# Two quarters of a token-major product turned back by DMA instead of on TensorE, and four squares moved behind their parts

## The chip, the cores and the metric

The kernel runs on one core of one Trainium2 chip. The metric is the device time of one execution in microseconds. Five engines work side by side, each through its own queue in order: TensorE (PE; its weight loads are shown as PEld), VectorE (DVE), ScalarE (ACT), GpSimd (POOL) and SyncE (SP), which here only issues DMAs. The order of the instructions in each queue is fixed when the program is built.

## The reference, cut to what matters

Two layers; each is a feed-forward block, a mixing block and a second feed-forward block, with a norm ahead of each and one at the end. All is float32, with 512 tokens, width 1024 and inner width 2816.

```python
def swiglu(h, w_gate, w_up, w_down):
    return (jax.nn.silu(h @ w_gate) * (h @ w_up)) @ w_down

for l in range(DEPTH):
    x = x + 0.5 * swiglu(rms_norm(x, ffn1_norm[l]), ffn1_wg[l], ffn1_wu[l], ffn1_wd[l])
    h = rms_norm(x, mix_norm[l])
    z = h @ w_in[l]
    ...            # window attention and short convolution of z
    x = x + jnp.concatenate([attn_out, conv_out], axis=-1) @ w_out[l]
    x = x + 0.5 * swiglu(rms_norm(x, ffn2_norm[l]), ffn2_wg[l], ffn2_wu[l], ffn2_wd[l])
return rms_norm(x, final_norm)
```

## The kernel before

**Layout.** The state `x` lies feature-major: eight blocks `xs[c]` of 128 features by 512 tokens, two of them to a tile `xpair[m]`. Every float32 factor is split into a high part (a cast to fp32r, on ScalarE) and a low part (the rest, by a subtraction on VectorE; line 223 does both), and a product is three matmuls: high by high, high by low, low by high. So weights come in by DMA as `raw`, become `wh` (ScalarE) and `wl` (VectorE), three buffers of each, and TensorE runs over them. `need_split` and `take_split` keep this up a fixed number of steps ahead, in the order of `plan()`.

**Seven products for eight.** The large products are taken in 2 x 2 blocks with seven block products instead of eight (`CHAINS`, `SHARES`). The feed-forward's stages are listed in `FIRST`, `INNER` and `LAST`: "p" and "w" make activations, "s" is a part of the down product (`share`) done by seven, and "d" a plain part of it (`down`). `INNER` is used by the second feed-forward of layer 0 and by the first of layer 1. It ends with two "s" stages and `("d", (9, 10))`.

**The product that lies apart.** In these "s" stages the result is token-major: `Apart.add` collects it in tiles `apart` (128 tokens by 512 features), and it must be turned before it can be added to `x`. It has four quarters `(o, t)`: feature half o, token half t. Two ways back are there:

- by DMA: `send` copies each of the two tiles of a quarter on ScalarE into `halves`, with the two 16-bit halves of the words laid apart (line 138), and issues one DMA transpose per tile on SP (line 901); `back` later copies the turned halves together on ScalarE, twice per quarter (line 914), and VectorE adds the result to `x` (line 918);
- on TensorE: `back` turns a quarter with eight transposes of 128x128 into PSUM (line 924), and VectorE adds it from there (line 929).

Before, quarters (0,0) and (1,1) go by DMA: sent behind steps 3 and 4 of the second "s" stage. Quarters (1,0) and (0,1) go over TensorE. Quarters (1,1) and (1,0) come back behind step 6, that is ahead of the "d" stage, and (0,0) and (0,1) behind its first block.

**The last "d" stage and the norm.** `down` yields the eight blocks of x in the order 4, 5, 6, 7, 0, 1, 2, 3, each after 12 matmuls. VectorE adds each to `xs[c]` (line 1318), and `after(c)` prepares the next norm: `take` makes the scaled high part (ScalarE, line 476) and low part (VectorE, line 477), `square` the square (ScalarE, lines 482 and 485) that VectorE accumulates in `nacc` (line 486). The norm's consumer starts with groups of 24 matmuls over the eight parts (line 321 to 324), in the same order of blocks, before the sum of squares is known; the split sum enters TensorE during the second group (`ssq`, line 542), and the root that comes of it scales the results afterwards. Behind the first site the results are gated, and their activation is split (`a`) for the next "d" stage; behind the second they become queries, keys and values.

What a line of Python issues is placed by a scheduler of the framework at build time, after its own estimates; `tc.issue_after` and `tc.manual_schedule` bind it. So the order on each engine can differ from the order of the source.

Of the kernel before, what the change touches and what calls it, by code (L numbers as in the profile page):

```python
# [16 lines left out]
P = 128  # L17
# [7 lines left out]
KC = D // P  # L25
NT = S // P
EPS = 1e-6
FAR = -3.0e38
H = S // 2
# [22 lines left out]
SHARES = ((0, 0, 1), (0, 0, 1), (1, 0, -1), (1, 1, 1), (1, 1, -1), (1, 0, 1), (0, 1, 1))  # L52


SENT_AT = {3: (0, 0), 4: (1, 1)}
SCORES_AT = (5, 6, 7, 8, 9, 10, 12, 13)
TURN_AT = (6, 7, 8, 10, 11, 12, 14, 15)
VALUES_AT = (7, 8, 9, 11, 12, 13, 15, 16)
# [14 lines left out]
def trunk_kernel(  # L73
# [23 lines left out]
    nc = tc.nc  # L97
# [8 lines left out]
    def psum(tag, shape, name):  # L106
        return ps.tile(shape, F32, tag=tag, bufs={"mm": 4, "sc": 2, "aux": 2}[tag], name=name)

    def g2(name, dt=F32, shape=(P, S)):
        return work.tile(list(shape), dt, tag="g2", bufs=14, name=name)  # L110
# [21 lines left out]
    def words(ap):  # L132

        return ap.bitcast(U16).rearrange("p (n two) -> p two n", two=2)
# [30 lines left out]
    ident = const.tile([P, P], F32, name="ident")  # L165
# [8 lines left out]
    def turn_rows(i):  # L174
        n = rows[i].shape[0]
        rp = psum("aux", [P, n], f"par_ps{i}")
        nc.tensor.transpose(rp, rows[i], ident[:n, :n])
        nc.scalar.copy(par[:, 16 * i : 16 * i + n], rp)
# [15 lines left out]
    state = {"raw": 0, "split": 0, "group": 0, "late": None}  # L194
# [153 lines left out]
    def halves_of(n, wide, last):  # L348

        blocks = list(range(0, n, wide))  # L350
        return blocks[len(blocks) // 2 :] + blocks[: len(blocks) // 2] if last else blocks

    def down(rhs, fresh=False, last=False):

        wide = abreast(len(rhs))
        for c in halves_of(KC, wide, last):
            n, hi, lo = take_split()
            if fresh and c == 0:
                yield from enumerate(level(n, hi, lo, rhs, wide))
                continue  # L360
            for j in range(wide):
                cols = slice(j * P, (j + 1) * P)
                own = (f"{n}_{j}", hi[:, :, cols], lo[:, :, cols])
                tag = ("sc", "sc", "aux", "aux")[j] if fresh else "mm"
                yield c + j, group(rhs, own=own, tag=tag)
# [515 lines left out]
    class Apart:  # L881
# [21 lines left out]
                    halves.rearrange("p a n -> p (a n)"),  # L903
                )

        def back(self, o, t, tag="mm"):

            for m in range(2 * o, 2 * o + 2):
                part = xpair[m][:, :, t * H : (t + 1) * H]
                if (o, t) in self.sent:  # L910
                    whole = g2(f"back_{self.name}_{m}_{t}")
                    j = 2 * (m - 2 * o)
                    with tc.issue_after(state["cast"]):
                        nc.scalar.copy(
                            words(whole).rearrange("p two (c s) -> p two c s", c=2),
                            self.sent[o, t][:, :, j : j + 2, :],
                        )
                    nc.vector.tensor_add(part, part, whole.rearrange("p (c s) -> p c s", c=2))
                    continue
                tp = psum(tag, [P, 2, H], f"back_{self.name}_{m}_{t}")  # L920
                for j in range(2):
                    c = (2 * m + j) % NT
                    for u in range(2):
                        nc.tensor.transpose(
                            tp[:, j, u * P : (u + 1) * P],
                            self.y[2 * t + u, o][:, c * P : (c + 1) * P],
                            ident,
                        )
                nc.vector.tensor_add(part, part, tp)

    def ahead(ops, at):
        return lambda step: ops.make(*at.get(step, ()))


    def ffn(norm, stages, after=None, late=None):
# [4 lines left out]
        def plain(b):  # L940
# [36 lines left out]
            acts[b] = (hi, lo)  # L977

        def winograd(b, between):


# [56 lines left out]
        def winograd2(b, between=None):  # L1038
# [14 lines left out]
            for step, (acc, operand, start) in enumerate(CHAINS):  # L1053
# [38 lines left out]
                if between:  # L1092
                    between(step)
# [115 lines left out]
        def shared(b):  # L1209
            return Seven(lambda: [raws[b], raws[b + 2]], room_form, f"s_{norm.i}_{b}")  # L1210

        def joined(between):


            def step(n):
                if n == 3:
                    crossing[0].join_half(0)
                if n == 4:
                    crossing.pop(0).join_half(1)
                if crossing and isinstance(crossing[-1], Tail):  # L1220
                    crossing[-1].during(n)
                between(n)

            return step
# [17 lines left out]
        def flush(n=1, *tag):  # L1242
            for _ in range(n):
                if pending:
                    pending.pop(0)(*tag)
# [3 lines left out]
        apart = None if first else Apart(f"{norm.i}")  # L1249
        for i, (what, b) in enumerate(stages):  # L1250
            if what in "wu" and stages[i + 1][0] == "s":
                ops = shared(sevens[0])
                if what == "w":
                    winograd2(b, ahead(ops, {3: ("b11",), 4: ("b21",), 5: ("t2",), 6: ("t3",)}))
                else:
                    winograd(b, ahead(ops, {1: ("b11",), 2: ("b21",), 4: ("t2",), 6: ("t3",)}))
            elif what == "w":
                if after is None and b == 1:
                    end = apart = Finale()
                winograd2(b, end and b == 1 and end.step)  # L1260
            if what == "s" and end:
                ends = [
                    Seven(full, None, f"e_{n}")
                    for n, full in enumerate((lambda b=b: [raws[b + 4], raws[b + 6]], raws[b + 8]))
                ]

                def between(step):
                    if 0 < step < 3:
                        flush(2, "mm")
                    for at, n, operand in ((3, 0, "b11"), (4, 1, "b11"), (5, 0, "t2"), (6, 1, "t2")):  # L1270
                        if step == at:
                            ends[n].make(operand)

                share(ops, 0.5, joined(between), apart, still=kept)
            elif what == "e":
                end.last(ends, kept)
                return
            elif what == "s" and b == sevens[0]:
                then = shared(sevens[1])
                share(  # L1280
                    ops,
                    0.5,
                    joined(ahead(then, {3: ("b11",), 4: ("b21",), 5: ("t2",), 6: ("t3",)})),
                    apart,
                    behind=(0, 2, 3) if first else (),
                    still=kept,
                )
            elif what == "s" and i + 1 == len(stages):
                share(then, 0.5, after.step, on=kept)
            elif what == "s":  # L1290

                def between(step):
                    if step in (2, 4):
                        with tc.issue_after(state["rest"]):
                            crossing[0].parts(step // 2 - 1)
                    if step in SENT_AT:
                        apart.send(*SENT_AT[step])
                    if step == 6:
                        apart.back(1, 1)
                        apart.back(1, 0, "aux")  # L1300

                share(then, 0.5, between, apart, behind=(0, 2, 3), on=kept)
            if what == "p":
                plain(b)
                if b == 0 and late:
                    turn_rows(1)
            if what != "d":
                continue
            rhs = [(acts[k][0][:, j, :], acts[k][1][:, j, :]) for k in b if k in acts for j in range(2)]
            final = i + 1 == len(stages)  # L1310
            if final:
                after.norm.order = halves_of(KC, 1, True)
            for c, acc in down(rhs, b == (0,) and not first, final):
                if b == (0,):
                    made = {0: "t3", 4: "t1"} if first else {0: "b21", 2: "t2", 5: "t3"}
                    if c in made:
                        norm.make(made[c])
                nc.vector.scalar_tensor_tensor(
                    xs[c], acc, 0.5, xs[c], op0=ALU.mult, op1=ALU.add
                )  # L1320
                flush()
                if final and c == KC // 2:
                    apart.back(0, 0)
                    apart.back(0, 1, "sc")
                if final:
                    after(c)
            if b == (0,) and first:
                norm.make("t4", "b22")
            if b == (1,) and late:
                late()  # L1330
# [426 lines left out]
```

## Time and profile before

| | us |
|---|---|
| median of 3 runs | 1648.56 (1648.53 to 1649.81) |
| profiled execution | 1648.68 |
| its span | 1646.9 |
| TensorE busy in the span | 1634.7 |
| VectorE busy | 1376.2 |
| ScalarE busy | 1107.6 |

A row of the timeline gives the start in us from the span's start, the duration, engine, line, operation and output<-input with their shapes; `x8` at its end means eight in one row, and a bracket tells how long the engine was idle before and for whom it waited. Instructions of VectorE and ScalarE overlap a little, so that the step from one start to the next is some 0.1 us shorter than the duration; TensorE's matmuls overlap more. In the view of one tile the figures behind a group are the least, median and greatest duration in ns, then the first and last start.

### The profile page before, as it was taken

What the parts mean: (1) busy time and instruction counts of PE and PEld (TensorE: products, weight loads), DVE (VectorE), ACT (ScalarE), POOL (GpSimd) and SP (SyncE); (2) the same over time, 40 slices, a digit from 0 to 9 for tenths busy, and PEclk for the clock granted to TensorE, in tenths of its full rate; (3) what the DMA queues carried; (4) which work ended last, traced back from release to release, by engine and by line L of the source; (5) the groups of instructions that cost most, each with busy time, mean ns of one, the idle gap of its engine ahead of it and who ended that gap; (6) DMA issues with size and microseconds to landing.
All of it is one profiled execution on the core that took longest, in us unless ns stands there. A gap on an engine that the chain in (4) does not pass through costs nothing.

```text
span 1646.9 us, 22039 instructions
## 1 busy us (share of the span) xinstructions
PE 1634.7 (99%) x8076; PEld 1380.4 (84%) x8076; DVE 1376.2 (84%) x1812; ACT 1107.6 (67%) x1453; POOL 212.3 (13%) x188
## 2 busy tenths in 40 slices
PE   9999999999999999999999999999999999999998
PEld 7888889988898888887888888878888988888886
DVE  7987779988899877797999777979788998777997
ACT  6447776566567577777665777776565766777665
POOL 0011111100221111111011111110012111111121
PEclk9999999999999999999999999999999999999999
DMA  8379997741397699999866999998124977999992
GB/s 256 83 199 212 221 245 186 175 126 52 105 235 176 176 216 218 214 204 236 217 151 177 219 216 225 213 230 204 52 65 129 231 152 186 220 224 224 234 262 70
DMA packets 277280, 306.10 MB, mean 186 GB/s; under 512 B 93804, under 2 KB 162484, under 8 KB 277172
## 3 DMA queue, kind: packets, MB, share of 16 engines
q1 hardware_dynamic: 236580, 222.24, 47.1%
q0 software_dynamic: 39872, 81.80, 28.8%
q8 instruction: 63, 1.03, 0.2%
q10 hardware_dynamic: 720, 0.66, 0.1%
q14 instruction: 45, 0.37, 0.1%
HBM read 262.71 MB, written 2.10 MB: 161 GB/s over the span
## 4 chain that ended last, share of the span: by engine, by line
PE 90%; DVE 5%; ACT 2%; issue 2%; DMA 1%; SPq 0%; DVEq 0%; ACTq 0%
PE x L827 25%; PE y L827 13%; PE acc L321 8%; PE acc L322 8%; PE acc L324 8%; PE w L827 6%; PE x_m L812 3%; PE x_s L827 3%; PE x_s L812 2%; DVE wl L223 2%; PE w_s L827 1%; PE y_s L812 1%; PE y_m L812 1%; PE y_e L827 1%; PE acc L707 1%
## 5 line engine op out<-in xcount | busy, mean ns | idle before, releaser
L223 ACT CAST wh<-raw 128x1024 fp32r<-128x1024 f32 (+1 forms) x491 | 510.9, 1044 | 367.6 <-PE x L827 91.9
L223 DVE TENSOR_TENSOR wl<-raw,wh 128x1024 fp32r<-128x1024 f32 (+1 forms) x491 | 594.5, 1219 | 174.6 <-ACT wh L223 173.6
L321 PE MATMUL acc<-xh,wh 128*128 128x512 f32 x424 | 165.8, 393 | 0.0
L322 PE MATMUL acc<-xl,wh 128*128 128x512 f32 x424 | 165.5, 390 | 0.0
L324 PE MATMUL acc<-xh,wl 128*128 128x512 f32 x416 | 162.3, 390 | 0.0
L218 POOL DMA_DIRECT2D raw<-in_ffn_wu_dram x39 | 48.7, 1248 | 400.0 <-DMA raw<-in_ffn_wu_dram 328.5
L322 PEld LDWEIGHTS acc<-xl,wh 128*128 128x128 f32 x424 | 79.7, 188 | 15.9 <-DVE xl L502 0.2
L321 PEld LDWEIGHTS acc<-xh,wh 128*128 128x128 f32 x424 | 79.8, 188 | 15.6
L324 PEld LDWEIGHTS acc<-xh,wl 128*128 128x128 f32 x416 | 78.1, 188 | 16.4
L218 POOL DMA_DIRECT2D raw<-in_ffn_wg_dram x39 | 48.3, 1264 | 222.9 <-DVE raw L262 70.8
L218 POOL DMA_DIRECT2D raw<-in_ffn_wd_dram x34 | 41.0, 1206 | 251.4 <-DMA raw<-in_ffn_wd_dram 80.4
L262 DVE TENSOR_TENSOR raw<-raw,raw 128x1024 f32<-128x1024 f32 x56 | 68.1, 1220 | 2.0 <-DMA raw<-in_ffn_wu_dram 1.1
L1158 ACT COPY raw_a<-turned 128x1024 uint16<-128x1024 uint16 x48 | 63.0, 1355 | 0.0
L827 PE MATMUL x<-wh,ft2h 128*128 128x512 f32 x152 | 59.2, 390 | 0.0
L827 PE MATMUL y<-wh,ft3h 128*128 128x512 f32 x152 | 59.2, 390 | 0.0
L827 PE MATMUL w<-wh,fb21h 128*128 128x512 f32 x152 | 59.2, 390 | 0.0
L827 PE MATMUL x<-wh,ft1l 128*128 128x512 f32 x152 | 59.2, 389 | 0.0
L827 PE MATMUL w<-wl,fb21h 128*128 128x512 f32 x152 | 59.2, 389 | 0.0
L827 PE MATMUL x<-wh,ft1h 128*128 128x512 f32 x152 | 59.2, 389 | 0.0
L827 PE MATMUL x<-wl,ft1h 128*128 128x512 f32 x152 | 59.2, 389 | 0.0
L827 PE MATMUL x<-wl,ft2h 128*128 128x512 f32 x152 | 59.2, 389 | 0.0
L827 PE MATMUL x<-wh,fb22l 128*128 128x512 f32 x152 | 59.2, 389 | 0.0
(607 smaller groups left out, 4625.0 us busy)
## 6 DMA issues: line engine op xcount, KB each, us to landing
raw<-in_ffn_wu_dram SPq DMA_DIRECT2D x126, 512.0 KB, 5.4
raw<-in_ffn_wd_dram SPq DMA_DIRECT2D x105, 512.0 KB, 6.2
raw<-in_ffn_wg_dram SPq DMA_DIRECT2D x86, 512.0 KB, 5.2
raw<-in_ffn_wu_dram POOLq DMA_DIRECT2D x39, 512.0 KB, 8.4
raw<-in_ffn_wg_dram POOLq DMA_DIRECT2D x39, 512.0 KB, 6.8
raw<-in_w_in_dram SPq DMA_DIRECT2D x36, 512.0 KB, 3.7
raw<-in_ffn_wd_dram POOLq DMA_DIRECT2D x34, 512.0 KB, 9.8
raw<-raw POOLq DMA_DIRECT2D x21, 512.0 KB, 7.0
```

Of the source, the lines that this page charges most:

```text
L218: nc.gpsimd.dma_start(out=r, in_=rows_of(*more), accum_op=ALU.add)
L223: return nc.scalar.copy(hi, raw), eng.tensor_sub(lo, raw, f32(hi))
L262: nc.vector.tensor_add(a11, a11, s1)
L321: nc.tensor.matmul(acc, hi[:, k, :], rhs[k][0], start=k == first, stop=False)
L322: nc.tensor.matmul(acc, hi[:, k, :], rhs[k][1], start=False, stop=False)
L324: nc.tensor.matmul(acc, lo[:, k, :], rhs[k][0], start=False, stop=k == last)
L707: nc.tensor.matmul(opening[n], (lo if part == "w" else hi)[:, k, :], xl if part == "x" else xh, start=n not in begun, stop=k == KC - 1 and ...
L812: nc.tensor.matmul(accs[c // 2][:, c % 2, :], w[:, k, cols], x_[:, 2 * h + k, :], start=start and c % 2 == 0 and h + k + i == 0, stop=h + ...
L827: nc.tensor.matmul(accs[u], x_[:, 2 * h + k, tok], w[:, k, :], start=start and h + k + i == 0, stop=h + k == 2 and i == 2, skip_group_chec ...
L1158: nc.scalar.copy(words(raws[self.b][:, c, :]), self.to[:, :, c, :])
```

## The change

All four quarters go by DMA. Quarter (1,0) is sent behind step 5 and (0,1) behind step 6. Only (1,1) still comes back ahead of the "d" stage; (1,0) comes back behind its block 5, (0,0) behind block 6, and (0,1) behind block 0. Blocks 4 and 5 are prepared for the norm behind block 5, blocks 6 and 7 each behind itself. For blocks 0 to 3 the source takes the scaled parts as each block is ready and the four squares only behind block 3.

```diff
-SENT_AT = {3: (0, 0), 4: (1, 1)}
+
+SENT_AT = {3: (0, 0), 4: (1, 1), 5: (1, 0), 6: (0, 1)}
+BACK_AT = {5: (1, 0), 6: (0, 0), 0: (0, 1)}
+FINAL_AT = {5: (4, 5), 6: (6,), 7: (7,)}
...
-        def back(self, o, t, tag="mm"):
+        def back(self, o, t):
 
             for m in range(2 * o, 2 * o + 2):
                 part = xpair[m][:, :, t * H : (t + 1) * H]
-                if (o, t) in self.sent:
-                    whole = g2(f"back_{self.name}_{m}_{t}")
...
-                    continue
-                tp = psum(tag, [P, 2, H], f"back_{self.name}_{m}_{t}")
-                for j in range(2):
-                    c = (2 * m + j) % NT
-                    for u in range(2):
-                        nc.tensor.transpose(
-                            tp[:, j, u * P : (u + 1) * P],
-                            self.y[2 * t + u, o][:, c * P : (c + 1) * P],
-                            ident,
-                        )
-                nc.vector.tensor_add(part, part, tp)
+                whole = g2(f"back_{self.name}_{m}_{t}")
+                j = 2 * (m - 2 * o)
+                with tc.issue_after(state["cast"]):
+                    nc.scalar.copy(
+                        words(whole).rearrange("p two (c s) -> p two c s", c=2),
+                        self.sent[o, t][:, :, j : j + 2, :],
+                    )
+                nc.vector.tensor_add(part, part, whole.rearrange("p (c s) -> p c s", c=2))
...
                     if step == 6:
                         apart.back(1, 1)
-                        apart.back(1, 0, "aux")
...
                 flush()
-                if final and c == KC // 2:
-                    apart.back(0, 0)
-                    apart.back(0, 1, "sc")
                 if final:
-                    after(c)
+                    if c in BACK_AT:
+                        apart.back(*BACK_AT[c])
+                    for k in FINAL_AT.get(c, ()):
+                        after(k)
+                    if c < KC // 2:
+                        after.norm.take(c)
+                    if c == KC // 2 - 1:
+                        for k in range(KC // 2):
+                            after.norm.square(k)
```

More of the change, by code (lines that the diff above doesn't have):

```diff
@@ L904, in send @@
                 )
-        def back(self, o, t, tag="mm"):
+        def back(self, o, t):
             for m in range(2 * o, 2 * o + 2):
                 part = xpair[m][:, :, t * H : (t + 1) * H]
-                if (o, t) in self.sent:
-                    whole = g2(f"back_{self.name}_{m}_{t}")
[L912 to L916, printed above, removed]
-                        )
-                    nc.vector.tensor_add(part, part, whole.rearrange("p (c s) -> p c s", c=2))
-                    continue
-                tp = psum(tag, [P, 2, H], f"back_{self.name}_{m}_{t}")
-                for j in range(2):
-                    c = (2 * m + j) % NT
-                    for u in range(2):
-                        nc.tensor.transpose(
-                            tp[:, j, u * P : (u + 1) * P],
-                            self.y[2 * t + u, o][:, c * P : (c + 1) * P],
-                            ident,
-                        )
-                nc.vector.tensor_add(part, part, tp)
+                whole = g2(f"back_{self.name}_{m}_{t}")
[6 more added lines that the diff above has]
+                nc.vector.tensor_add(part, part, whole.rearrange("p (c s) -> p c s", c=2))
     def ahead(ops, at):
```

## The prediction

> **What bounds the kernel now.** I read the page first, then the waits of TensorE, then the two stages that the change touches by the windows and the timeline of each engine. The page's first lines:
>
> ```profile
> span 1646.9 us, 22039 instructions
> ...
> PE 1634.7 (99%) x8076; PEld 1380.4 (84%) x8076; DVE 1376.2 (84%) x1812; ACT 1107.6 (67%) x1453; POOL 212.3 (13%) x188
> ```
>
> TensorE is busy for 99% of the span, so what leaves TensorE leaves the time, unless a wait takes its place. The largest wait of TensorE in the view of waits (who waited, for whom, total us, times, longest) is small:
>
> ```profile
> PE x_s L827 <- ACT wh L223: 1.3, 4, 0.5
> ```
>
> The changed code runs twice: in the second "s" stage, the last "d" stage and the next norm of layer 0's second feed-forward and of layer 1's first. I call these the two sites; the first begins at 805.3 us, the second at about 1132, as the first and last starts of the transposes show:
>
> ```profile
> L924 PE MATMUL back<-ident,apart x32: 270/272/273, 805.3 to 1135.6; 128*128 128x128 f32 x32
> L914 ACT COPY back<-turned x8: 1342/1353/1366, 804.9 to 1136.2; 128x1024 uint16<-128x1024 uint16 x8
> ```
>
> Two windows of the first site (length, then busy us of PE, PEld, DVE, ACT, POOL, granted clock, DMA share, GB/s) say what else is tight there:
>
> ```profile
> 798.00:806.00 8.00, 8.00 (x40) 6.66 (x40) 7.01 (x8) 5.24 (x6) 0.00 (x0) 1.00 1.15 286
> 806.00:829.00 23.00, 23.00 (x109) 19.18 (x107) 21.58 (x31) 15.27 (x21) 0.00 (x0) 1.00 0.47 140
> ```
>
> TensorE never stops at full clock. But VectorE is busy for 21.58 of 23 us, and ScalarE has under 8 us left. These two prepare the norm that TensorE takes up next.
>
> **What is removed: 32 transposes on TensorE.** Eight for each of two quarters, at two sites. Their price is read from the starts around one group of eight:
>
> ```profile
> 805.06 0.39 PE L827 MATMUL x_s<-wl,fb22h_s 128*128 128x512 f32 x1
> 805.30 1.03 PE L924 MATMUL back<-ident,apart 128*128 128x128 f32 x8
> 806.09 0.48 PE L321 MATMUL acc<-ah,wh 128*128 128x512 f32 x1
> 806.40 0.40 PE L322 MATMUL acc<-al,wh 128*128 128x512 f32 x1
> ```
>
> From 805.06 to 806.40 are 1.34 us; two ordinary matmuls in that place take two steps of 0.227 us (from 828.84 to 851.08, in rows quoted below, TensorE issues 98 of them in 22.24 us). So a group costs 0.88 us, and four groups 3.5 us. TensorE has no gap at this place, so all of it counts: -3.5.
>
> The Trainium skill ("VectorE: DVE Perf Modes", The three transpose paths and Rules for kernel authors) speaks against this change: for a 128x128 block it gives 390 ns on TensorE and 1309 ns through the DMA crossbar, and advises TensorE wherever PSUM will do as the destination. By its 390 ns the 32 transposes would be worth 12.5 us, an estimate from that page; the trace's 0.88 us for eight is 3.5 us, and the sum goes by the trace.
>
> **What is added.** Each new quarter brings two re-layout copies to halves on ScalarE, two DMA transposes on SP's queue and two copies back on ScalarE: per site 4, 4 and 4. VectorE's adds stay the same in number, only their source moves from PSUM to SBUF (0.69 beside 0.68 us), which is nothing. ScalarE's steps, start to start:
>
> ```profile
> 798.11 1.99 ACT L138 COPY halves<-apart 128x1024 uint16<-128x1024 uint16 x2
> ...
> 804.86 2.58 ACT L914 COPY back<-turned 128x1024 uint16<-128x1024 uint16 x2 [1.26 <-DMA turned<-halves]
> 807.31 1.03 ACT L223 CAST wh<-raw 128x1024 fp32r<-128x1024 f32 x1
> 808.24 2.58 ACT L914 COPY back<-turned 128x1024 uint16<-128x1024 uint16 x2
> ...
> 828.88 0.72 ACT L476 ACTIVATE xh<-x,par 128x512 fp32r<-128x512 f32 x1 [2.01 <-DVE x L1318]
> 829.51 0.62 ACT L485 ACTIVATE nsq<-x 128x512 f32<-128x512 f32 x1
> 830.03 0.71 ACT L476 ACTIVATE xh<-x,par 128x512 fp32r<-128x512 f32 x1
> ```
>
> A pair of halves takes 1.9 us, a pair of copies back 2.45 (a single one 1.22), a weight cast 0.94, a scaled part 0.63, a square 0.52. The added 8.7 us per site (two pairs of halves, two pairs back) exceed the nearly 8 us that ScalarE had idle in the window, although one pair of halves falls before it. So ScalarE, and behind it VectorE, becomes as long as the "d" stage itself.
>
> I walk the first site in the order of the changed program. Z is 805.3, where the blocks of the "d" stage now begin; eight blocks of 12 matmuls end at E = Z + 8 x 12 x 0.227 = Z + 21.8. ScalarE's last pair of halves waits for the last two adds into the token-major sums. Before, one of these began at 804.77, the other at 806.86 behind an add that is now gone:
>
> ```profile
> 804.77 0.68 DVE L894 SCALAR_TENSOR_TENSOR apart<-x_s,apart 128x512 f32<-128x512 f32 x1
> ...
> 809.27 1.22 DVE L223 TENSOR_TENSOR wl<-raw,wh 128x1024 fp32r<-128x1024 f32 x1
> 810.41 0.68 DVE L1318 SCALAR_TENSOR_TENSOR x<-acc,x 128x512 f32<-128x512 f32 x1
> ...
> 826.90 0.75 DVE L477 SCALAR_TENSOR_TENSOR xl<-x,par,xh 128x512 fp32r<-128x512 f32 x1
> 827.56 0.69 DVE L486 TENSOR_TENSOR nacc<-nacc,nsq 128x512 f32<-128x512 f32 x1
> 828.16 0.68 DVE L1318 SCALAR_TENSOR_TENSOR x<-acc,x 128x512 f32<-128x512 f32 x1
> ```
>
> The pair can start between Z+0.2 (804.77 + 0.68) and Z+1.4; I take Z+1.0, because the other new pair of halves has delayed a weight cast, and its subtraction on VectorE stands ahead of these adds. From there ScalarE has, one behind the other: halves 1.9; back (1,1) and (1,0) 4.9; cast 0.94; parts and squares of blocks 4 and 5, 2.3; back (0,0) 2.45; block 6, 1.15; cast 0.94; one copy of back (0,1) 1.22; part of block 7, 0.72. That is 16.5, so Z+17.5. VectorE then has, at steps of 0.66 (low part), 0.60 (accumulate or add) and 1.14 (weight subtraction): low part 7, accumulate, block 0's result, two back adds, a subtraction, low part 0, results of blocks 1 and 2: 6.1, so block 3's result starts at Z+23.6. Behind it, with the squares moved to the end: 0.60, accumulate 0.60, three low parts 1.98, accumulate 0.60, subtraction 1.14, accumulate 0.60, subtraction 1.14, last accumulate 0.69, the cast of the sum on ScalarE 0.62: 8.0. The sum of squares is ready at Z+31.6. TensorE asks for it after 39 matmuls of the norm, at E + 8.85 = Z+30.65. So TensorE loses **1.0 us per site**, in part already at the low part of block 1, in part at the sum. The bounds: 0.2 (start at Z+0.2) to 1.4. At the second site the same instructions stand in the same order.
>
> Behind the first site alone comes a second wait. The next stage's first product needs the first activation's cast on ScalarE, and the following weight cast needs a buffer that TensorE frees with the last but one matmul of the norm's groups. Before, the activation (849.09) stands ahead of that weight cast (851.09) in ScalarE's queue:
>
> ```profile
> 849.09 0.62 ACT L223 CAST a<-gate 128x512 fp32r<-128x512 f32 x1
> 851.09 1.06 ACT L228 CAST wh<-raw 128x1024 fp32r<-128x1024 f32 x1 [1.38 <-issue]
> ```
>
> ```profile
> 828.84 0.39 PE L321 MATMUL acc<-xh,wh 128*128 128x512 f32 x1
> ...
> 850.62 0.39 PE L322 MATMUL acc<-xl,wh 128*128 128x512 f32 x1
> 850.85 0.39 PE L324 MATMUL acc<-xh,wl 128*128 128x512 f32 x1
> 851.08 0.39 PE L340 MATMUL acc<-a,wh 128*128 128x512 f32 x1
> ```
>
> In the changed program the two have changed places. The weight cast starts 0.01 us after TensorE could go on (851.09 against 851.08), the activation 0.95 later, its 0.62 and a hand-over of some 0.05 follow: TensorE waits **1.6 us**, however early the rest is.
>
> **The transposes' landing.** Nothing so far holds ScalarE for a transfer. Back (1,0) is wanted at Z+1.0+1.9+2.45 = Z+5.3 = 810.6. SP before:
>
> ```profile
> 799.17 3.29 SPq L901 DMA_TRANSPOSE turned<-halves  x2
> 802.56 1.14 SPq L206 DMA_DIRECT2D raw<-in_ffn_wu_dram  x2
> 803.80 1.83 SPq L206 DMA_DIRECT2D raw<-in_ffn_wd_dram  x2
> ```
>
> and over all transposes, issue to landing:
>
> ```profile
> DMA to landing us min/median/max: 2.7/5.1/11.1
> ```
>
> The new pair stands where the load at 803.80 stood; its second transpose issues 1.2 to 2 us later and at the median 5.1 lands at 810.1 to 810.9; with the DMA share at 1.15 until 806, up to 1.4 us more is likely. I take 0.7 us late per site, and it passes on nearly in full, since neither ScalarE nor VectorE has room before the norm: +1.4. The last pair, (0,1), is wanted only at Z+15 and costs nothing; without that cover it would cost what it is late. The weight loads behind the four transposes go out some 2.5 to 6 us later; the DMA share of 0.47 after 806 is room for them, and I cost them at nothing (uncovered, up to those 6 us).
>
> **The sum.** -3.5 + 2 x 1.0 + 1.6 + 1.4 = +1.5 us. The profiled execution took 1648.68 us, its span 1646.9 and 1.8 around it, near the median 1648.56. So 1648.68 + 1.5 = **1650.2 us**: no change that a measurement tells, which here is about 0.2% or 3.3 us (below 1645.3 or above 1651.9).
>
> **The rivals.**
>
> *The waits do not come* (0.08). If VectorE and ScalarE catch up, the sum of squares costs nothing: -3.5 + 1.6 = 1646.8, still within 0.2%; only with the activation in time as well is it 1645.2 and faster. For it: TensorE loses almost nothing before. Against it: the order of the queue, and 21.58 us of VectorE in 23.
>
> *The transposes land late* (0.36). ScalarE stands at back (1,0), everything behind it on ScalarE waits, VectorE's adds wait for it, and the norm's parts are late by as much. The point that decides: past about 1.6 us late per site the total exceeds 3.3 us. At 3 us late (8.1 from issue to landing, midway from the median to the longest row): -3.5 + 2 x 4.0 + 1.6 = +6.1, 1654.8. For it: a share of 1.15 as these are issued, four transposes in a row of loads, and 3.29 us of SP for one pair. Against it: the share falls to 0.47 afterwards. The advice of the page named above, to stay on TensorE, points to this side as well.
>
> *The change does not act*: excluded, as the changed program has 32 matmuls fewer and 8 DMA transposes more.
>
> **How the numbers follow.** The forecast has 0.56, its own range 1647.2 (0.2 at each sum and no late landing: -3.5 + 0.4 + 1.6 = -1.5) to 1651.9. The range to both sides: 1646.8, without the wait at the sum, to 1654.8, with landings 3 us late. Faster by over 0.2%: 0.08; within: 0.56; slower: 0.36.
>
> **What would show it.** After: no transposes at the two sites; TensorE with waits for VectorE's low part and ScalarE's cast of the sum, together near 1 us at each site, and about 1.6 us at the first product behind the first site; ScalarE without idle time from 806 to about 823. Wrong would be the forecast if ScalarE idles for microseconds at back (1,0) (then slower), or if TensorE passes both norms without a wait (then faster).

## The result, and the profile after

The changed kernel takes 1651.63 us (median; 1650.81 to 1655.28) against 1648.59 us before in the same measurement: a ratio of 1.0022, 95% interval 1.0015 to 1.0029, so +3.0 us. It is slower by 0.18%, 1.4 us above the 1650.2 forecast. That is 0.3 us inside the 1651.9 up to which the prediction spoke of no change that a measurement tells; the interval leaves 1 out, so this measurement does tell it. The profiled execution took 1651.41 us, its span 1649.6.

The page of the changed kernel, its span and busy times:

```profile
span 1649.6 us, 22011 instructions
...
PE 1632.8 (99%) x8044; PEld 1376.3 (83%) x8044; DVE 1376.2 (83%) x1812; ACT 1124.2 (68%) x1469; POOL 213.1 (13%) x188
```

TensorE has 32 instructions fewer and ScalarE 16 more, 16.6 us of them. Its waits (who waited, for whom, total us, times, longest) show where the time went; three of these rows are new, and two of them stand above the largest of before (1.3 us):

```profile
PE acc L325 <- DVE xl L480: 2.1, 2, 1.1
PE acc L343 <- ACT a L226: 1.5, 1, 1.5
PE x_s L830 <- ACT wh L226: 1.3, 4, 0.5
...
PE ssq L545 <- ACT sqh L226: 1.0, 2, 0.5
```

The low part of block 1 (line 325) and the sum of squares (line 545) are waited for at both sites, the first product (line 343) behind the first site only. The view gives the idle time before the instruction. What TensorE really loses is the step from the matmul before, less an ordinary step of 0.227 us. TensorE's timeline at the three places of the first site:

```profile
830.12 0.39 PE L324 MATMUL acc<-xh,wh 128*128 128x512 f32 x1
831.45 0.50 PE L325 MATMUL acc<-xl,wh 128*128 128x512 f32 x1 [0.94 <-DVE xl L480]
831.79 0.40 PE L327 MATMUL acc<-xh,wl 128*128 128x512 f32 x1
...
836.62 0.39 PE L327 MATMUL acc<-xh,wl 128*128 128x512 f32 x1
837.50 0.50 PE L545 MATMUL ssq<-sqh,ones_r 128*128 128x512 f32 x1 [0.50 <-ACT sqh L226]
...
850.81 0.39 PE L327 MATMUL acc<-xh,wl 128*128 128x512 f32 x1
852.67 0.50 PE L343 MATMUL acc<-a,wh 128*128 128x512 f32 x1 [1.47 <-ACT a L226]
```

So the low part costs 1.33 - 0.23 = 1.1 us, the sum 0.65 and the first product 1.63. At the second site the same two waits of the norm cost 1.3 and 0.67. Behind each wait the steps stay longer for a few matmuls: 831.45 to 831.79 is 0.34 instead of 0.227.

ScalarE from the end of the "s" stage, and SP's queue beside it (timelines):

```profile
806.01 2.00 ACT L141 COPY halves<-apart 128x1024 uint16<-128x1024 uint16 x2
807.91 2.56 ACT L916 COPY back<-turned 128x1024 uint16<-128x1024 uint16 x2
811.25 2.57 ACT L916 COPY back<-turned 128x1024 uint16<-128x1024 uint16 x2 [0.78 <-DMA turned<-halves]
```

```profile
803.08 4.42 SPq L904 DMA_TRANSPOSE turned<-halves  x2
```

ScalarE stands 0.78 us at back (1,0) for a transfer that was issued from 803.08 on and has landed by 811.25. The two windows of the site (length, busy us of PE, PEld, DVE, ACT, POOL, clock, DMA share, GB/s) show the rest:

```profile
806.00:829.00 23.00, 23.00 (x104) 19.03 (x103) 19.33 (x28) 21.47 (x26) 0.00 (x0) 1.00 0.75 176
829.00:852.00 23.00, 20.75 (x89) 16.14 (x87) 19.41 (x29) 16.05 (x20) 4.22 (x4) 1.00 0.62 146
```

ScalarE is busy for 21.47 us of 23 where it was 15.27, and half of the 1.5 us left is the wait for that transfer. VectorE is busy for less than before, 19.33 us for 21.58: its adds stand waiting for ScalarE's copies (6.6 us over both sites), and its work moves into the window behind. TensorE pays in the window behind it: 20.75 us of 23.

### The profile page after: what moved, and what is told of

Same layout as the page of the kernel before. It is cut to its first block, busy times and chain, and to the rows that moved or that the text cites. A ratio compares the mean times of both kernels' runs of the same rounds, so it can differ in the third digit from the quotient of the medians.

```text
span 1649.6 us, 22011 instructions
## 1 busy us (share of the span) xinstructions
PE 1632.8 (99%) x8044; PEld 1376.3 (83%) x8044; DVE 1376.2 (83%) x1812; ACT 1124.2 (68%) x1469; POOL 213.1 (13%) x188
## 3 DMA queue, kind: packets, MB, share of 16 engines
q8 instruction: 63, 1.03, 0.2%
## 4 chain that ended last, share of the span: by engine, by line
PE 86%; DVE 6%; ACT 3%; DMA 3%; issue 2%; SPq 0%; DVEq 0%; ACTq 0%
PE x L830 25%; PE y L830 13%; PE acc L325 7%; PE acc L324 7%; PE acc L327 6%; PE w L830 6%; PE x_m L815 3%; PE x_s L830 3%; PE x_s L815 2%; DVE wl L226 2%; DMA turned<-halves 2%; PE y_s L815 1%; PE y_m L815 1%; PE y_s L830 1%; PE w_s L830 1%
## 5 line engine op out<-in xcount | busy, mean ns | idle before, releaser
L830 PE MATMUL y<-wh,ft4h 128*128 128x512 f32 x152 | 59.3, 390 | 0.1
L830 PE MATMUL w<-wh,fb21l 128*128 128x512 f32 x152 | 59.2, 389 | 0.0
L830 PE MATMUL x<-wh,ft2l 128*128 128x512 f32 x152 | 59.2, 389 | 0.0
```

Source lines behind the costliest of these rows:

```text
L830: nc.tensor.matmul(accs[u], x_[:, 2 * h + k, tok], w[:, k, :], start=start and h + k + i == 0, stop=h + k == 2 and i == 2, skip_group_chec ...
```

## The experiments

Each was timed against the kernel before in the same measurement (1648.6 to 1648.8 us); what is said below of the changed kernel compares with its 1651.63 us, from a measurement of its own.

**The price of the transposes.** The kernel before, without the two quarters that TensorE turns and without VectorE's adds of them:

```diff
                     continue
+                continue
                 tp = psum(tag, [P, 2, H], f"back_{self.name}_{m}_{t}")
```

> The kernel before without the two quarters that TensorE turns: the transposes and their additions to x are left out, so x lacks these quarters. It measures the removal by itself: 4 x 0.88 = 3.5 us less by the step of the prediction, 1645.2. If TensorE's 0.27 us for a transpose were not hidden in part (32 x 0.27), 8.7 us less; if the norm's preparation waits anyway for VectorE, under 2 us less.

1645.38 us (ratio 0.9977, 0.9967 to 0.9987), 3.4 us less, and no new wait. The term of -3.5 stands.

**The late squares alone.** The kernel before, with the squares of blocks 0 to 3 behind block 3's part:

```diff
-                    after(c)
+                    after.norm.take(c)
+                    if c >= KC // 2:
+                        after.norm.square(c)
+                    if c == KC // 2 - 1:
+                        for k in range(KC // 2):
+                            after.norm.square(k)
```

> The kernel before with the other half of the change alone: two quarters still turned on TensorE, the squares of blocks 0 to 3 behind block 3's part. If the late squares cost something only because ScalarE and VectorE are already behind, there is no change: 1648.6 and no new wait of TensorE (before, the cast of the sum was ready 2.7 us ahead of TensorE). If the late squares are the cause by themselves, TensorE waits about 1 us per site and the time is 1650.6.

1648.61 us (ratio 1.0, 0.9991 to 1.0009), no new wait. ScalarE is busy for 15.57 us of the 23, the first activation's cast stays ahead of the third weight pair (848.47 and 850.47 us), and the move is free.

**The squares with their blocks, in the changed kernel.**

```diff
-                        after.norm.take(c)
-                    if c == KC // 2 - 1:
-                        for k in range(KC // 2):
-                            after.norm.square(k)
+                        after(c)
```

> The changed kernel, but each of blocks 0 to 3 is squared right behind its scaled part, as before. If the wait behind the first site hangs on the late squares (they put the accumulates, the sum and the root late, and the scheduler then puts a weight cast ahead of the activation's cast), both the wait for the cast of the sum (0.5 us at each site) and the 1.6 us at the first product go, some waiting moves to the low parts, and the time falls by about 1.8 us from 1651.6 to 1649.8. If the squares' place does not matter and only the added copies on ScalarE do, it stays at 1651.6.

1649.76 us (ratio 1.0007, 0.9998 to 1.0015), 1.9 us below the changed kernel. TensorE's waits at the norm:

```profile
PE acc L325 <- DVE xl L480: 1.8, 4, 0.6
...
PE acc L324 <- ACT xh L479: 0.9, 1, 0.9
```

The wait for the sum is gone, and the one at the first product too; the parts of the blocks, now behind the squares on ScalarE, are waited for longer. The idle time at the norm falls only from 3.1 to 2.7 us, and by the steps nothing is gained there: six waits cost 4.0 us over both sites where the changed kernel's four cost 3.8. With this edit ScalarE's order behind the norm comes out differently as well; the first activation's cast stands ahead of the third weight pair, as it did before:

```profile
849.93 0.61 ACT L226 CAST a<-gate 128x512 fp32r<-128x512 f32 x1
```

The gain of 1.9 us is thus the wait at the first product (1.63 us by its step) and a small one that followed it at 886.6 us (0.22). So the late squares cost nothing at the norm itself. Beside the added copies they cost 1.9 us through an order that they bring about elsewhere.

**The quarter that landed first is brought back first.** (0,0), sent behind step 3, comes back with (1,1) ahead of the "d" stage:

```diff
-BACK_AT = {5: (1, 0), 6: (0, 0), 0: (0, 1)}
+BACK_AT = {5: (1, 0), 0: (0, 1)}
...
                         apart.back(1, 1)
+                        apart.back(0, 0)
```

> The changed kernel, but quarter (0,0), whose transposes were sent long before, comes back right behind (1,1), ahead of (1,0); the number of instructions is the same. If ScalarE's 0.8 us of idle time at (1,0) is the landing of its transposes and passes on to TensorE, it vanishes, TensorE's waits at the low part of block 1 (1.1 and 1.3 us) go, and about 2 to 2.8 us fall away: 1649 to 1649.6. If ScalarE's amount of work alone sets the lateness, it stays at 1651.6.

1649.38 us (ratio 1.0004, 0.9995 to 1.0013), 2.2 us below the changed kernel. ScalarE's timeline shows six copies in a row, none held by a transfer; of TensorE's waits the low part's is gone, the sum's has grown from 1.0 to 1.5 us, and the first product's stays:

```profile
807.35 7.42 ACT L916 COPY back<-turned 128x1024 uint16<-128x1024 uint16 x6
```

```profile
PE ssq L545 <- ACT sqh L226: 1.5, 2, 0.8
PE acc L343 <- ACT a L226: 1.5, 1, 1.5
```

By the steps, the sum now costs 0.93 us at each site and the low part nothing: 1.9 us at the norms instead of 3.8. So about 1.1 us per site went with the late landing; the edit also moves four copies ahead of ScalarE's casts and parts, so the split between landing and order is argued, not shown.

**Both repairs together** (the two diffs above):

> Both repairs in the changed kernel: quarter (0,0) comes back ahead of (1,0), and blocks 0 to 3 are squared right behind their parts. If the late landing (2.2 us in the run with the first repair) and the late squares (1.9 us in the run with the second) are separate terms, both fall away and what stays is a wait at the low parts of near 1 us per site: 3.0 - 2.2 - 1.9 = 1.1 us below before, 1647.5. If they are the same lateness counted twice, the time stays near 1649.4.

1647.49 us (ratio 0.999, 0.9982 to 0.9999), 4.1 us below the changed kernel: the two gains of 2.2 and 1.9 add up. It has every instruction of the changed kernel, and it is 1.3 us below the kernel before. Of the 3.5 us that the transposes are worth 2.2 are still lost; one row of the norm is left among the waits, and by the steps four waits cost 1.55 us:

```profile
PE acc L325 <- DVE xl L480: 0.8, 3, 0.3
```

**The wait at the first product: the order on ScalarE.** The prediction put it down to the third weight cast, which stands ahead of the first activation's cast. First the weight cast was queued behind that cast:

```diff
+                ahead_of = state.pop("act", None)
+                with tc.issue_after(ahead_of) if ahead_of else nullcontext():
+                    sent = split_far(hi, lo, raw)
-                sent = split_far(hi, lo, raw)
```

> The changed kernel with one order bound: the third weight cast of the next stage stands behind the first activation's cast on ScalarE, as before the change. If the 1.6 us at the first product come of these two having changed places, as the prediction has it, they go: 1650.0. If the activation's own inputs are late as well (the root came late, and a cast that waits for VectorE now stands ahead of the activation), TensorE still waits about 1.6 us there and the time stays at 1651.6.

1651.27 us (ratio 1.0014, 1.0005 to 1.0023), and the wait stays at 1.5 us. Another cast had moved into the place (ScalarE's timeline):

```profile
851.55 1.04 ACT L226 CAST fb21h<-hf 128x1024 fp32r<-128x1024 f32 x1 [1.80 <-DVE hf L561]
852.50 0.61 ACT L226 CAST a<-gate 128x512 fp32r<-128x512 f32 x1
```

Then both were queued behind it, the weight cast as above and the cast of that operand with it:

```diff
-                        norm.make(made[c])
+                        held = state.get("first_act") if c == 0 and not first else None
+                        with tc.issue_after(held) if held else nullcontext():
+                            norm.make(made[c])
```

> The changed kernel with the first activation's cast bound ahead of both casts that stood before it on ScalarE, the weight cast and that of the next operand. If the order on ScalarE is the cause of the 1.6 us behind the first site, TensorE waits there no longer and the time is 1650.0. If VectorE's product that the cast reads is itself late (it began at 851.43 us where TensorE wanted the activation at about 851.5), a wait of 1.2 to 1.4 us stays and the time is within 0.4 us of 1651.6.

1652.92 us (ratio 1.0023, 1.0012 to 1.0035): no gain that can be measured. In the timelines of VectorE, ScalarE and TensorE the wait shrinks from 1.63 to 1.31 us (850.94 to 852.48, less 0.227):

```profile
851.09 0.68 DVE L947 TENSOR_TENSOR gate<-acc,gate 128x512 f32<-128x512 f32 x1
```

```profile
851.80 0.62 ACT L226 CAST a<-gate 128x512 fp32r<-128x512 f32 x1 [2.40 <-DVE gate L947]
```

```profile
850.94 0.39 PE L329 MATMUL acc<-xh,wl 128*128 128x512 f32 x1
852.48 0.50 PE L345 MATMUL acc<-a,wh 128*128 128x512 f32 x1 [1.15 <-ACT a L226]
```

Nothing stands ahead of the activation any more, and still it is late, because VectorE's product (851.09) is. A second place in the order makes that one late. ScalarE's timeline of the changed kernel, behind the root:

```profile
843.66 0.63 ACT L937 ACTIVATE gate<-gate 128x512 f32<-128x512 f32 x1
845.79 1.06 ACT L230 ACTIVATE wl<-raw 128x1024 fp32r<-128x1024 f32 x1 [1.50 <-PE acc L327]
846.76 1.03 ACT L231 CAST wh<-raw 128x1024 fp32r<-128x1024 f32 x1
847.70 0.63 ACT L937 ACTIVATE gate<-gate 128x512 f32<-128x512 f32 x1
...
851.05 1.04 ACT L231 CAST wh<-raw 128x1024 fp32r<-128x1024 f32 x1 [1.78 <-issue]
852.00 0.61 ACT L226 CAST a<-gate 128x512 fp32r<-128x512 f32 x1
```

The second gate activation (847.70) stands behind a weight pair that waits 1.5 us for a buffer of TensorE. In the kernel before, the two gates came one behind the other:

```profile
843.49 1.15 ACT L946 ACTIVATE gate<-gate 128x512 f32<-128x512 f32 x2
```

Two runs separate the two places. The first binds the weight pair (`far_of[-1]`) behind the second gate, and changes nothing else on ScalarE:

```diff
+                silu = gate(accs[1])
+                if not first:
+                    for i in far_of[-1]:
+                        tc.add_manual_dep(
+                            i.ins,
+                            silu.name,
...
-                gate(accs[1])
```

> The changed kernel with one instruction of ScalarE moved at the first site: the second gate activation is issued right behind the first, ahead of the weight pair whose buffer TensorE frees at 845.8 us; before this edit it stood behind that pair. VectorE's product, which begins at 850.95 us in the changed kernel, should come about 1.2 us earlier. Theory one: two places in ScalarE's order each make the first activation's cast late by themselves, this one and the third weight cast that stands ahead of the activation's cast (851.05 us). Then the wait at the first product stays at 1.5 to 1.6 us, since the third weight cast still holds the activation's cast until 852.0 us, and the time stays at 1651.3 to 1652. Theory two: the gate alone makes it late. Then the wait falls below 0.6 us and the time to about 1650.3. Theory three: the late root of the norm makes everything late, whatever the order; then VectorE's product doesn't move.

1651.88 us (ratio 1.002, 1.0011 to 1.0029), and the wait at the first product stays 1.63 us (860.26 to 862.12). This one profiled execution lost 9.4 us from 753 us on to a late weight and a halved clock, outside the sites, so its times stand later by as much. VectorE's product now ends 0.7 us before the third weight cast, and the activation's cast is held by that cast alone:

```profile
859.10 0.69 DVE L947 TENSOR_TENSOR gate<-acc,gate 128x512 f32<-128x512 f32 x1
```

```profile
860.50 1.04 ACT L232 CAST wh<-raw 128x1024 fp32r<-128x1024 f32 x1 [2.31 <-issue]
861.45 0.61 ACT L226 CAST a<-gate 128x512 fp32r<-128x512 f32 x1
```

The second run makes both edits of the order:

> Both edits of ScalarE's order at the first site in the changed kernel: the second gate activation right behind the first, and the first activation's cast ahead of the third weight cast and of the cast of the b21 operand (the latter alone left a wait of 1.31 us). Theory one (two places, each enough by itself): VectorE's product begins near 849.8 us, the activation's cast near 850.5 us, before TensorE asks for it at about 851.1 us; the wait at the first product is gone or below 0.2 us, and the time is about 1650.0. Theory three (the root's lateness): TensorE still waits 1 us or more at the first product, and the time stays at 1651 to 1652.

The wait is gone: the step into the first product is an ordinary one.

```profile
853.31 0.39 PE L330 MATMUL acc<-xh,wl 128*128 128x512 f32 x1
853.54 0.50 PE L346 MATMUL acc<-a,wh 128*128 128x512 f32 x1
```

Each of the two places alone makes the activation late, by 1.63 and by 1.31 us; only without both is it in time, although the root is as late as in the changed kernel (it starts 12.07 us ahead of the first product's turn in both). The median, 1651.29 us (ratio 1.0017, 1.0008 to 1.0026), is 0.3 below the changed kernel instead of the 1.6 expected. The interval is 1.5 us to either side and holds both, so the time doesn't show the gain. The profiles do: compared start by start with that of before, TensorE loses 3.0 us net between 797 and 1230 us in the changed kernel and 1.6 in this one.

**GpSimd makes the copies back.** If ScalarE's load is what costs, another engine should take it:

```diff
-                with tc.issue_after(state["cast"]):
-                    nc.scalar.copy(
+                nc.gpsimd.tensor_copy(
```

> The changed kernel with the eight copies back of each site on GpSimd, which does nothing between 798 and 829 us, instead of ScalarE. If ScalarE's amount of work makes the norm late, and GpSimd copies 128x1024 16-bit values in 1.5 to 2.5 us each, the waits at both norms and at the first product shrink to under 1 us together and the time is 1645.5 to 1648. If the landing of the transposes is all that counts, the time stays at 1650 to 1651.6. If GpSimd takes over 4 us for a copy, its eight copies outlast the stage and the time is above 1653.

1662.49 us (ratio 1.0073, 1.0059 to 1.0086), 10.9 us above the changed kernel: a miss, though GpSimd's copies take 1.34 to 2.35 us each, as the first theory asked. The same with both repairs:

> The copies back on GpSimd, quarter (0,0) ahead of (1,0), and each block squared behind its part. With GpSimd's copies at 1.5 to 2.5 us each, no wait of TensorE is left at either site and the whole price of the transposes is gained: 3.5 us, 1645.2. If GpSimd's copies are slow (over 4 us), they are the new chain and the time is above 1650.

1655.46 us (ratio 1.0034, 1.0022 to 1.0047), a miss as well, 8.0 us above the same kernel with ScalarE's copies. What both theories had left out is seen in the timelines of GpSimd and VectorE (the second of these kernels):

```profile
804.04 11.00 POOL L915 COPY back<-turned 128x1024 uint16<-128x1024 uint16 x6 [23.99 <-DMA turned<-halves]
816.87 3.92 POOL L915 COPY back<-turned 128x1024 uint16<-128x1024 uint16 x2 [1.82 <-DMA turned<-halves]
```

```profile
811.14 2.70 DVE L919 TENSOR_TENSOR x<-x,back 128x512 f32<-128x512 f32 x2
813.76 0.68 DVE L1308 SCALAR_TENSOR_TENSOR x<-acc,x 128x512 f32<-128x512 f32 x1
814.36 2.38 DVE L919 TENSOR_TENSOR x<-x,back 128x512 f32<-128x512 f32 x3
...
817.80 3.48 DVE L480 SCALAR_TENSOR_TENSOR xl<-x,par,xh 128x512 fp32r<-128x512 f32 x2
```

While GpSimd copies (until 815.04, and from 816.87), VectorE's adds with two operands in SBUF take 1.35 us each instead of 0.69, its low parts 1.74 instead of 0.74. The add at 813.76 reads one operand from PSUM and keeps its 0.68; the three at 814.36, mostly behind the copies, are nearly back at theirs. GpSimd's own copies take 1.83 us each (11.00 for six) against ScalarE's 1.22. VectorE was busy for 21.58 of 23 us before, so the load has moved to where it hurts more. How much of the loss is this contention and how much GpSimd's longer copies was not separated. The Trainium skill ("SBUF — State Buffer", Who interferes with whom) states this case: a VectorE instruction with two SBUF inputs contends with a GpSimd instruction that reads SBUF, one with at most one SBUF input, outside the 2-port performance modes, doesn't. The trace agrees, with these numbers.

**Half of the change.** The kernel before, with (0,1) by DMA, sent behind step 6 and brought back behind block 0; (1,0) stays on TensorE, and the squares with their blocks:

```diff
-SENT_AT = {3: (0, 0), 4: (1, 1)}
+SENT_AT = {3: (0, 0), 4: (1, 1), 6: (0, 1)}
...
-                    apart.back(0, 1, "sc")
+                if final and c == 0:
+                    apart.back(0, 1)
```

> Half the change: three quarters by DMA, (1,0) still on TensorE, (0,1) sent behind step 6 and back behind block 0, squares as before. It removes 16 transposes (1.75 us) and adds to ScalarE 2 pairs of copies per site where the whole change adds 4. If the lateness comes of ScalarE and VectorE being filled past the length of the stage, half the load stays below that point: no wait of TensorE at either site, 1648.7 - 1.75 = 1647.0. If lateness grows in proportion to the load, half the waits come as well (2.9 us of 5.9) and the time is 1650.

1646.62 us (ratio 0.9987, 0.9978 to 0.9996), the lowest median of the kernels that leave nothing out: 2.2 us below the kernel before, 5 below the changed one. TensorE waits at neither site. ScalarE's busy time in the window is 20.45 us, one below the changed kernel's:

```profile
806.00:829.00 23.00, 23.00 (x106) 19.15 (x105) 21.11 (x31) 20.45 (x25) 0.00 (x0) 1.00 0.83 178
```

The two groups of transposes removed are worth 1.76 us by the price above; the rest of the 2.2 lies within the interval. More than the load differs from the changed kernel here: the squares stay with their blocks, and no copy of ScalarE stands waiting for a transfer. The nearer comparison is the kernel with both repairs. It has all four quarters, ScalarE is busy for 21.48 us of the same window, and its waits cost 1.55 us; here, with 20.45, there are none. The two times are 0.9 us apart and their intervals overlap.

## Why the prediction came out as it did

**The sign and the places were right.** The 32 transposes are worth 3.4 us measured alone, against 3.5. TensorE waits where the walk said: at the low part of block 1, at the sum of squares, and at the first product behind the first site. ScalarE's last pair of halves begins 1.05 us behind the first block of the "d" stage (806.01; the block's first matmul at 804.96) where 1.0 was taken, and it stands 0.78 us at back (1,0), 1.03 at the second site, where 0.7 was taken.

**The size was off by 1.5 us.** The waits at the norm were forecast as 1.0 for the order and 0.7 for the landing, 3.4 us over both sites. They measure 1.11 + 0.66 and 1.32 + 0.67, 3.8 us. The term that was too small is the landing, as far as the runs can tell: with its repair 0.93 us per site is left, near the 1.0 for the order, and the time falls by 2.2 us, 1.1 per site, not 0.7. The first product is 1.63 against 1.6. Two things were not in the sum at all. A wait of 0.2 us comes at 886.6. And each wait is followed by longer steps: compared start by start with the profile of before, the changed kernel's matmuls lose 6.5 us in all at and behind the sites (and gain 3.5 at the transposes); the steps into the six waits make 5.6 of it, so those behind them cost 0.9, or 0.15 us per wait. 0.4 + 0.2 + 0.9 are the missing 1.5 us.

**Load and order.** The walk has ScalarE, and behind it VectorE, become as long as the "d" stage. ScalarE does (21.47 us of 23); VectorE's work in the window shrinks, and it is late because it waits for ScalarE's copies. Nor is the lateness the amount of work alone: the two repairs remove no instruction and win back 4.1 of the 6.5 us. The late squares, which the walk put into the norm's sum, cost at the first product instead.

**The first product: right in size, but not the only cause.** The step that "the two have changed places" is shown sufficient: with the other cause removed (gates together) the weight cast alone still costs 1.63 us. What failed is what it implied, that their order is the cause. With their order put right (act first), 1.31 us stayed, from the second gate activation that the walk had not followed: it stopped at the sum of squares. Nor is the late root the cause: with both places put right it is as late and the wait is gone.

**The rivals.** Transposes that land 3 us late did not come; 0.78 us did. The waits' absence did not come either; of the kernels with more quarters by DMA only the one with half the load has none.

**The page's advice.** The Trainium skill ("VectorE: DVE Perf Modes", Rules for kernel authors) advises TensorE where PSUM will do. The outcome of the whole change agrees, but not by that page's price: eight transposes are worth 0.86 us here (3.4 for 32). The page's prices are for bf16 blocks; these are float32. What decided were the copies on ScalarE that each DMA transpose brings along and their order: with half of them, or with all of them in a better order, the DMA is ahead.

## What to carry to other kernels

Work taken from a full engine is paid in the stage where its helpers do the replacement: sum the helpers' instructions in that stage against its length, and leave room for their own waits (with ScalarE busy for 20.45 us of 23 TensorE never waited, with 21.48 it did; one quarter moved gained 2.2 us, two lost 3.0, and with both repairs gained 1.3). A full helper is only half of it: 4.1 us hung on the order of the same instructions. Bring back first what was sent first, and re-examine an order that was harmless while there was slack. When a fix of an order changes nothing, look for a second place that suffices alone, and test both together.

## What the runs showed of the hardware

GpSimd's copies (1.34 us at the least, 1.83 beside VectorE) and VectorE's instructions with two SBUF inputs slow each other, as shown above. The other surprise is the clock. In the first kernel with GpSimd's copies TensorE waits four times within 6 us at the norm (timeline), and then its granted clock is halved (windows of 1 us, columns as above):

```profile
835.22 0.51 PE L324 MATMUL acc<-xh,wh 128*128 128x512 f32 x1 [0.57 <-ACT xh L479]
836.33 0.50 PE L325 MATMUL acc<-xl,wh 128*128 128x512 f32 x1 [0.60 <-DVE xl L480]
...
837.59 0.50 PE L325 MATMUL acc<-xl,wh 128*128 128x512 f32 x1 [0.30 <-DVE xl L480]
...
839.99 0.80 PE L325 MATMUL acc<-xl,wh 128*128 128x512 f32 x1 [1.04 <-DVE xl L480]
840.58 0.63 PE L327 MATMUL acc<-xh,wl 128*128 128x512 f32 x1
841.01 0.63 PE L324 MATMUL acc<-xh,wh 128*128 128x512 f32 x1
```

```profile
838.00:839.00 1.00, 0.82 (x3) 0.19 (x1) 1.00 (x2) 0.91 (x2) 0.00 (x0) 1.00 0.00 0
...
840.00:841.00 1.00, 1.00 (x2) 0.81 (x3) 0.90 (x2) 0.18 (x1) 0.00 (x0) 0.50 0.63 80
```

The matmuls behind take steps of 0.43 us, twice the ordinary one, for some 3 us; so this kernel lost more than its waits. The Trainium skill ("TensorE: Matmul & The Clock Gate", HAM oscillation — how this bites in real kernels) gives as its rule to leave no idle gaps beyond about 3.4 us. Here the clock fell with no gap over about 1.3 us, so short ones close together can be enough. They need not be: in the second of these kernels TensorE waits 0.65, 0.60 and 0.28 us at the first site and the clock is halved from 835.3 us on, while after 0.64, 0.60, 0.30 and 0.29 us at the second site it stays at 1.00. What decides between the two is not shown. In the changed kernel the two waits of a norm lie 6 us apart, and the clock stays at 1.00.
